# A two-block transformer on one core: paired small experts in the mixture, an early bias table, and the value product of the key memory turned round

## The chip, the cores and the metric

One core of one Trainium2 chip runs the whole program. The metric is the device time of one execution in microseconds (us). Three executions were timed, and one was profiled. TensorE does the matrix products (PE in the profile, PEld its weight loads), VectorE (DVE) and ScalarE (ACT) the elementwise work, GpSimd (POOL) small things and gathers, SyncE (SP) starts most transfers.

## What is computed

512 tokens of width 1024 go through two blocks. Block 1: modulation and norm, input products, retention and differential attention, output product, then a mixture of 32 experts (width 512), of which each token goes to two, weighted by its gates:

```python
for expert e, its tokens x:
    y = (silu(x @ w_gate[e]) * (x @ w_up[e])) @ w_down[e]
    out[token] += gate * y
```

Block 2: norm, a windowed attention with 8 heads, to whose scores a table of biases by relative position is added, a pooling branch, an output product, and last a key memory of 16384 entries with vectors u and v:

```python
a = gelu(h @ u.T) * weight      # weight is 0 but for the chosen entries
out = x + a @ v
```

## The kernel before, in words

Data is fp32. An operand of a large product is cut in two parts, `hi` (rounded to the type fp32r of TensorE) and `lo` (the rest), and three products are summed: hi·hi, hi·lo and lo·hi. A weight comes in chunks of 128x1024 (512 KB) through one ordered list (`add`, from L612). The class `Stream` (`pump`, L338) starts each chunk's load on SP's queue as soon as one of the raw buffers is free (L352), and a given number of chunks ahead of use ACT copies the `hi` part (L363) and DVE subtracts the `lo` part (L365). Each of these engines works through its instructions in order, so an engine that waits for a chunk holds everything behind it. The eight PSUM banks go through `B.get` and `B.put`. Work beside the large products is written as generators (`side`): each `tick` inside a product lets up to two of them go one step.

The helpers are `mm` and `mmx` (products, L522 and L526), `tt` (L529), `stt` (L532), `ts` (L536, L538), `acp` (a copy or function on ACT, L541) and `tr` (a transpose on TensorE, L544). In the profile every use of a helper has its line.

**Block 1's output product** (from L1196) multiplies in chunks (`go(MG, ev_x1, j)`). Beside it run the generators `shift_rows` (pushed at L1230) and `rows_of`, one for each finished tile, which uses ACT and TensorE. Meanwhile `Stream` loads and cuts the first chunks of the experts.

**The mixture** (L1463 to L1690) ranks experts by their number of tokens; rank z is a place. `block_rows(z)` (L119) is a bound on the tokens of a place: 128 for places 0 and 1 and for 29 to 31 (which have two such blocks), between 40 and 128 for the others. `STEPS` (L111) gives the order: by falling rank, with the three large places at steps 6, 13 and 20. A step is `gate_up` (8 chunks), `turn` of the next place (its token rows transposed, split), `down` of the place before (4 chunks), `turn_a`. The token rows are the stationary operand and the weight moves, 512 columns a time: 72 products for each block of rows, however few the rows. `scatter` (L1522) scales the result by the gates (`gtab`) and writes it to memory through POOL.

**The start of block 2** (L1700 to L1785). `band_bias` (L1765) multiplies the bias table by a 0/1 matrix of buckets, and POOL writes the 8x511 result to memory, each row 128 times (L1771, `lb_d`, 2 MB). POOL then reads it back with a pitch that shifts each row by one (L1773, `bmv`), and DVE adds the band mask ten ticks on. `norms` (L1700) needs POOL too, for a power of the norm's statistics (L529 by way of `power`).

**The key memory's product** (L2400 to L2500) goes by 32 groups of 512 entries (`SEQ` is their order), for the first 384 tokens; the other 128 tokens are done by gathers on POOL and sums on DVE (L2291, L2308, L532). For half of the groups `a` is held from an earlier stage, for the other half `u_block` makes it here (24 products of 384 columns for 128 entries, then Gelu on ACT); `weigh` multiplies by the weights and splits. `v_group` (L2437) has the v chunk stationary and the tokens moving: in each half of the width four banks collect 4 blocks of 128 entries, 96 products of 384 columns a group, and DVE adds each of the 8 banks to `X4` (which holds x and becomes the output).

## Time and profile before

| | us |
|---|---|
| median of three timed executions | 2932.4 (2931.6 to 2934.65) |
| the profiled execution, its own time | 2930.98 |
| its span, first to last instruction | 2929.2 |
| PE busy in the span | 2726.5 (93%) |
| DVE busy | 2238.9 (76%) |
| ACT busy | 1262.3 (43%) |
| POOL busy | 757.6 (26%) |

How to read the rows below. A row of the timeline has the start in us, the duration, engine, line and operation, output and inputs, shape and count, and in brackets how long the engine was idle before and what it waited for. A row of the view by line has the busy time, the mean ns of one instruction, and the idle time before them with what ended it. [...] A row of the view of waits has who waited for whom: us in total, times, longest. Pipelined products overlap in their ends, so the time that one adds is read from the distance of two starts.

### The profile page before, as it was taken

The numbers are of one execution on the slowest core, as the hardware profiler recorded it, in microseconds if no ns is written. First come the engines' busy times: TensorE is split into PE (matmuls) and PEld (weight loads), VectorE is DVE, ScalarE is ACT, GpSimd is POOL, SyncE is SP. The second block draws the span as 40 slices with busy tenths as digits, with TensorE's granted clock in tenths as the row PEclk, the third lists the DMA queues.
The fourth block names the chain that finished last, engine by engine and source line by source line (L and its number), as shares of the span: only waits on it lengthen the run. The fifth ranks groups of instructions, "written<-read, shape, count | busy, mean of one in ns | idle before, by whom it ended". The sixth has DMA issues, their size and how long they took to land.

```text
span 2929.2 us, 40594 instructions
## 1 busy us (share of the span) xinstructions
PE 2726.5 (93%) x14351; PEld 2342.7 (80%) x14351; DVE 2238.9 (76%) x4096; ACT 1262.3 (43%) x1859; POOL 757.6 (26%) x669
## 2 busy tenths in 40 slices
PE   6999999988999999985799988999999999999999
PEld 5887888877877665544567888899899999999999
DVE  7554566548898878863558998999688888888887
ACT  3432344345676766751334233444333333333332
POOL 6110021111212111101424555222132332333231
PEclk8999999998999999996899999999999999999999
DMA  6546322347998989975223335888989989999895
GB/s 221 165 124 208 130 73 72 119 140 248 351 323 320 341 305 334 353 247 113 68 69 113 97 118 186 294 293 295 306 296 300 306 287 311 296 297 312 283 304 187
DMA packets 242211, 673.83 MB, mean 230 GB/s; under 512 B 26497, under 2 KB 94513, under 8 KB 238288
## 3 DMA queue, kind: packets, MB, share of 16 engines
q1 hardware_dynamic: 176224, 467.14, 47.3%
q0 software_dynamic: 48256, 156.44, 15.9%
q10 hardware_dynamic: 17520, 47.57, 4.5%
q8 instruction: 115, 1.88, 0.3%
q14 instruction: 96, 0.79, 0.1%
HBM read 625.27 MB, written 62.06 MB: 235 GB/s over the span
## 4 chain that ended last, share of the span: by engine, by line
PE 49%; DVE 29%; DMA 7%; issue 7%; ACT 7%; POOL 1%; ACTq 0%; DVEq 0%; POOLq 0%; SPq 0%
PE bank L522 44%; DVE lo L365 7%; DVE arena L529 6%; DVE arena L532 4%; ACT hi L363 4%; DVE arena L2308 3%; PE bank L526 3%; PE bank L544 2%; DVE arena L538 2%; DVE arena_r L529 2%; ACT arena_r L541 2%; DMA lb_d<-arena 2%; DMA raw<-in_w_in_dram 1%; DMA raw<-in_w_ret_o_dram 1%; ACT arena L541 1%
## 5 line engine op out<-in xcount | busy, mean ns | idle before, releaser
L522 PE MATMUL bank<-arena_r,hi 128*128 128x384 f32 (+1 forms) x5792 | 1618.5, 360 | 42.0 <-DVE arena L529 29.0
L522 PEld LDWEIGHTS bank<-arena_r,hi 128*128 128x128 f32 x5792 | 1066.6, 192 | 123.2 <-issue 39.0
L522 PE MATMUL bank<-arena_r,lo 128*128 128x384 f32 (+1 forms) x2896 | 1032.1, 356 | 22.3 <-POOL lo L365 15.9
L365 DVE TENSOR_TENSOR lo<-raw,hi 128x1024 fp32r<-128x1024 f32 x490 | 602.7, 1242 | 219.9 <-ACT hi L363 215.1
L522 PEld LDWEIGHTS bank<-arena_r,lo 128*128 128x128 f32 x2896 | 554.2, 191 | 65.0 <-POOL lo L365 18.5
L363 ACT ACTIVATE hi<-raw 128x1024 fp32r<-128x1024 f32 x513 | 523.5, 1051 | 176.7 <-DMA raw<-in_v_dram 56.4
L541 ACT ACTIVATE arena<-bank 128x512 f32<-128x512 f32 (+7 forms) x478 | 251.2, 535 | 569.6 <-PE bank L522 437.7
L522 PE MATMUL bank<-hi,arena_r 128*128 128x512 f32 (+10 forms) x1064 | 346.2, 396 | 7.5 <-DVEq L2548 6.2
L541 ACT ACTIVATE arena_r<-arena 128x384 fp32r<-128x384 f32 (+1 forms) x160 | 87.5, 547 | 495.1 <-DVE arena L529 447.9
L529 POOL TENSOR_TENSOR arena<-arena 128x512 f32<-128x512 f32 (+10 forms) x172 | 180.8, 1069 | 380.3 <-ACT arena L541 274.3
L2291 POOL DMA_INDIRECT arena<-in_ur_dram,idx_i x128 | 156.0, 1219 | 401.0 <-DVE arena L2308 393.4
L2291 POOL DMA_INDIRECT arena<-in_vr_dram,idx_i x128 | 157.2, 1228 | 362.6 <-DVE arena L532 337.5
L522 PE MATMUL bank<-arena_r 128*128 128x512 f32 (+12 forms) x956 | 232.9, 398 | 4.4 <-DVE arena_r L538 4.4
L522 PEld LDWEIGHTS bank<-hi,arena_r 128*128 128x128 f32 (+10 forms) x1064 | 161.5, 152 | 89.9 <-issue 7.9
L529 DVE TENSOR_TENSOR arena<-arena,bank 128x384 f32<-128x384 f32 (+6 forms) x314 | 167.9, 570 | 72.3 <-PE bank L522 72.1
L522 PE MATMUL bank<-lo,arena_r 128*128 128x512 f32 (+10 forms) x532 | 209.2, 393 | 1.3 <-DVE lo L365 1.3
L522 PEld LDWEIGHTS bank<-arena_r 128*128 128x128 f32 (+10 forms) x956 | 151.4, 162 | 70.9 <-issue 4.3
L1530 POOL DMA_INDIRECT y_d<-arena,dst_i x34 | 53.0, 1558 | 502.1 <-ACT hi L363 212.4
L529 DVE TENSOR_TENSOR arena_r<-arena,arena_r 128x384 fp32r<-128x384 f32 (+1 forms) x160 | 94.6, 591 | 103.4 <-ACT arena_r L541 103.3
L532 DVE SCALAR_TENSOR_TENSOR arena<-arena 128x1024 f32<-128x1024 f32 (+3 forms) x136 | 165.5, 1217 | 0.2
L2308 DVE SCALAR_TENSOR_TENSOR arena<-arena 128x1024 f32<-128x1024 f32 x128 | 156.0, 1219 | 0.0
L529 DVE TENSOR_TENSOR arena<-arena 128x384 f32<-128x384 f32 (+8 forms) x272 | 125.3, 481 | 23.6 <-DMA arena<-g_d 9.9
(171 smaller groups left out, 2827.1 us busy)
## 6 DMA issues: line engine op xcount, KB each, us to landing
raw<-in_u_dram SPq DMA_DIRECT2D x128, 512.0 KB
raw<-in_v_dram SPq DMA_DIRECT2D x128, 512.0 KB
raw<-in_w_down_dram SPq DMA_DIRECT2D x72, 512.0 KB
raw<-in_w_gate_dram SPq DMA_DIRECT2D x70, 512.0 KB
raw<-in_w_up_dram SPq DMA_DIRECT2D x68, 512.0 KB
arena<-in_w_up_dram SPq DMA_DIRECT2D x60, 512.0 KB
arena<-in_w_gate_dram SPq DMA_DIRECT2D x58, 512.0 KB
raw<-in_w_in_dram SPq DMA_DIRECT2D x57, 512.0 KB
```

Source lines behind the costliest of these rows:

```text
L363: self.nc.scalar.activation(h, r, AF.Copy)
L365: e.tensor_tensor(l, r, h.bitcast(F32), op=OP.subtract)
L522: pe.matmul(ps, l, r, start=start, stop=stop)
L526: pe.matmul(ps, l, r, start=start, stop=stop, skip_group_check=True)
L529: e.tensor_tensor(o, x, y, op=op)
L532: dve.scalar_tensor_tensor(o, x, s, y, op0=op0, op1=op1)
L538: (e or dve).tensor_scalar(o, x, s1, s2, op0=op0, op1=op1)
L541: act.activation(o, x, f, **kw)
L544: pe.transpose(ps, x, kk("ident")[:n, :n])
L1530: i = pool.indirect_dma_start(out=y_d[:], out_offset=IOA(ap=dst_i[:r, z:z + 1], axis=0), in_=y[:r], in_offset=None, bounds_check=2 * S - 1 ...
L2291: pool.indirect_dma_start(out=b, out_offset=None, in_=a[tab], in_offset=IOA(ap=idx_i[:, j:j + 1], axis=0))
L2308: dve.scalar_tensor_tensor(b, b, 1.0, h3, op0=OP.mult, op1=OP.mult, accum_out=s_[:, j:j + 1])
```

## The change

Four things change.

1. The order of the places: after 0 and 1, places of few and of many tokens take turns, `STEPS` is [0, 1, 14, 2, 15, 3, 31, 16, 4, 17, 5, 18, 6, 19, 30, 7, 20, 8, 21, 9, 22, 10, 23, 29, 11, 24, 12, 25, 13, 26, 27, 28]; before it was 0 to 5, 31, 6 to 11, 30, 12 to 17, 29, 18 to 28.
2. The 15 places 14 to 28 get a block of exactly 64 rows, and `hi` and `lo` of the rows stand side by side as 128 columns of the stationary operand. For a piece of a chunk there are two products in place of three. The two halves of the result's 128 rows are added by `fold` (eight small products) behind the gate and up products, and by DVE in `scatter`.
3. The bias table is made in block 1's output product (`bias_rows`, ahead of `shift_rows` among the generators), and the 2 MB write to `lb_d` goes on SP's queue. Block 2 only reads it back, on ACT's queue.
4. In the key memory's product the tokens are stationary and v moves, 512 columns a time: 72 products of 512 columns a group. Six banks hold the output of the 384 tokens through all 32 groups, and two banks are left for `u_block`. x goes into the banks first (`residual_in`, 24 products with the identity, from `x4_d` loaded on ACT's queue). The 8 adds of a group are gone; at the end 6 banks are copied out. Rows of v are laid out in their own order, and the output's layout changes with it.

```diff
 NG = 32
 SEQ = _order()
 RG = 8
...
     if z < NSTAT or z >= NE - NBIG:
         return P
-    return min(P, -(-(2 * S // (z - NSTAT + NBIG + 1)) // RG) * RG)
+    r = min(P, -(-(2 * S // (z - NSTAT + NBIG + 1)) // RG) * RG)
+    return r if r > HB else HB
+
+
...
+    put("fold", (p % HB)[:, None] == np.arange(HB)[None, :])
...
+        def bias_rows():
+
+            lrow, relb = get(), sm(8)
+            nc.sync.dma_start(lrow[:32, :511], a["buckets"])
+            nc.sync.dma_start(relb[:32], a["relb"])
+            for _ in range(4):
+                yield
+            ps = B.get()
+            mm(ps[:8, :511], relb[:32], lrow[:32, :511], True, True)
+            yield
+            acp(lrow[:8, :511], ps[:8, :511])
+            B.put(ps)
+            pool.memset(lrow[:8, 511:512], 0.0)
+            yield
+            nc.sync.dma_start(lb_d[:], lrow[:8, :].unsqueeze(1).to_broadcast([8, P, 512]))
+            lrow.put()
+
         xg = [get(2, True) for _ in range(3)]
...
-        side.push(shift_rows())
+        side.push(bias_rows(), shift_rows())
         ss, lg = B.get(), B.get()
 
...
+        def beside(o, x, n):
+
+            v = o.rearrange("p (q k r) -> p q k r", k=2, r=HB)
+            x = x.rearrange("p (q r) -> p q r", r=HB)
+            acp(v[:, :, 0, :], x)
+            tt(dve, v[:, :, 1, :], x, v[:, :, 0, :].bitcast(F32), OP.subtract)
+
+        def mm_pair(ps, x, wh, wl, first, last):
+
+
+            mmx(ps, x, wh, first, last)
+            mmx(ps[:HB], x[:, :HB], wl, False, last)
+
...
+
+                ps = B.get()
+                for q in range(KT):
+                    tr(ps[:, q * r:(q + 1) * r], x[:r, q * P:(q + 1) * P], r)
+                t = getr(2)
+                beside(t.ap, ps, KT)
+                B.put(ps)
+                xts[z] = t
+                return
...
+        def gate_up_pair(z):
+            x = xts.pop(z)
+            t = []
+            for k in range(2):
+                ps = B.get()
+                for q in range(4):
+                    j, wh, wl = W.get()
+                    for s in range(2):
+                        i = 2 * q + s
+                        c = slice(512 * s, 512 * s + 512)
+                        mm_pair(ps, x[:, i * P:(i + 1) * P], wh[:, c], wl[:, c], i == 0, i == KT - 1)
+                    W.done(j)
+                    tick()
+                y = get()
+                if k:
+                    dve.tensor_copy(y.ap, ps)
+                else:
+                    acp(y.ap, ps)
+                B.put(ps)
+                t.append(y)
+            x.put()
+            act_t[z] = t
+
...
+                    for q in range(4):
+                        o = (4 * k + q) * r
+                        mm(ps[:, o:o + r], y[:, q * P:(q + 1) * P], kk("fold"), True, True)
+                    y.put()
+                y, o = get(), getr()
+                acp(y[:, :256], ps[:, :256], AF.Silu)
+                tt(dve, y[:, :256], y[:, :256], ps[:, 256:], OP.mult)
+                B.put(ps)
+                beside(o.ap, y[:, :256], 4)
+                y.put()
+                aT[z] = o
+                return
             for q in range(4):
                 tr(ps[:, q * r:(q + 1) * r], t[:r, q * P:(q + 1) * P], r)
             t.put()
...
-            ts(y[:r, 512:], o[1][:r], gtab[:r, z:z + 1])
+            if paired(z):
+                for n in range(2):
+                    c = y[:r, 512 * n:512 * n + 512]
+                    acp(c, o[n][HB:], AF.Copy, scale=gtab[HB:, z:z + 1])
+                    stt(c, o[n][:r], gtab[:r, z:z + 1], c, OP.mult, OP.add)
+            else:
+                acp(y[:r, :512], o[0][:r], AF.Copy, scale=gtab[:r, z:z + 1])
+                ts(y[:r, 512:], o[1][:r], gtab[:r, z:z + 1])
...
         bmv = bm.ap.rearrange("p (h c) -> p h c", h=8)
-        onb, relb, lrow, band = get(), get(), get(), get()
-        nc.scalar.dma_start(onb[:32, :511], a["buckets"])
-        nc.scalar.dma_start(relb[:32, :8], a["relb"])
+        band = get()
+        lb = lb_d[:]
+        nc.scalar.dma_start(bmv, bass.AP(tensor=lb.tensor, offset=lb.offset + 127,
+                                         ap=[[511, P], [P * 512, 8], [1, 256]]))
         nc.scalar.dma_start(band[:, :256], a["band"])
         sk = sm(8)
...
-            ps = B.get()
-            mm(ps[:8, :511], relb[:32, :8], onb[:32, :511], True, True)
-            pool.memset(lrow[:8, 511:512], 0.0)
-            acp(lrow[:8, :511], ps[:8, :511])
-            B.put(ps)
-            pool.dma_start(lb_d[:], lrow[:8, :].unsqueeze(1).to_broadcast([8, P, 512]))
-            lb = lb_d[:]
-            pool.dma_start(bmv, bass.AP(tensor=lb.tensor, offset=lb.offset + 127,
-                                        ap=[[511, P], [P * 512, 8], [1, 256]]))
-            yield
             for _ in range(10):
                 yield
             tt(dve, bmv, bmv, band[:, :256].unsqueeze(1).to_broadcast([P, 8, 256]), OP.add)
-            put([onb, relb, lrow, band])
+            band.put()
             ready.append(1)
 
...
+        for n in range(2):
+            nc.scalar.dma_start(xl[n].ap, flat(x4_d[:, 4 * n:4 * n + 4]))
         eslot = get(3, tight=True).ap
...
+
+        acc = [[B.get() for _ in range(2)] for _ in range(ND // P)]
+
+        def residual_in():
+
+            for t, bs in enumerate(acc):
+                for q in range(KT):
+                    x = xl[q // 4][:, q % 4 * ND + t * P:q % 4 * ND + t * P + P]
+                    mmx(bs[q // 4][:, q % 4 * P:q % 4 * P + P], x, kk("ident"), q % 4 == 0, False)
+                tick()
+            put(xl)
+
+        def v_block(x, last):
+
+            c = W.get()
+            for t in range(ND // P):
+                xh, xl_ = (z[:, t * P:(t + 1) * P] for z in x)
+                for n in range(2):
+                    h, l = (z[:, n * 512:n * 512 + 512] for z in c[1:])
+                    ps = acc[t][n]
+                    mmx(ps, xh, h, False, False)
+                    mmx(ps, xl_, h, False, False)
+                    mmx(ps, xh, l, False, last)
+                    if last:
+                        y = get()
+                        if n:
+                            acp(y.ap, ps)
+                        else:
+                            dve.tensor_copy(y.ap, ps)
+                        oc = t * D + n * 512
+                        (nc.sync, nc.scalar)[n].dma_start(out[:, oc:oc + 512], y.ap)
+                    if not (n and t == 1):
+                        if (t, n) != (2, 1):
+                            tick()
+            W.done(c[0])
+            put(x)
 
         load_gate(0)
         load_ge()
...
             if i == 0:
-                for n in range(2):
-                    nc.sync.dma_start(X4[n], flat(x4_d[:, 4 * n:4 * n + 4]))
+                residual_in()
...
-                v_group(w_c, i == NG - 1)
+                for b, x in enumerate(w_c):
+                    v_block(x, i == NG - 1 and b == 3)
```

## Rows read from the trace of the kernel before

**Rows 1.** The page: busy time of the engines, and the chain that ended last.

```profile
PE 2726.5 (93%) x14351; PEld 2342.7 (80%) x14351; DVE 2238.9 (76%) x4096; ACT 1262.3 (43%) x1859; POOL 757.6 (26%) x669
...
PE 49%; DVE 29%; DMA 7%; issue 7%; ACT 7%; POOL 1%; ACTq 0%; DVEq 0%; POOLq 0%; SPq 0%
```

**Rows 2.** [...]

```profile
675.00:1313.00 638.00, 627.72 (x2951) 422.21 (x2950) 532.82 (x567) 447.32 (x554) 107.92 (x101) 0.99 0.88 319
696.00:1236.00 540.00, 540.00 (x2556) 373.71 (x2554) 461.59 (x480) 386.58 (x480) 100.07 (x90) 1.00 0.90 332
...
912.00:948.00 36.00, 36.00 (x176) 28.15 (x175) 24.46 (x28) 19.68 (x26) 10.20 (x4) 1.00 0.75 272
...
1164.00:1200.00 36.00, 36.00 (x171) 18.76 (x170) 32.34 (x35) 26.85 (x34) 4.01 (x6) 1.00 0.98 359
```

**Rows 3.** The timeline of TensorE in two steps of small places.

```profile
1176.93 5.71 PE L522 MATMUL bank<-arena_r 128*48 128x512 f32 x24
...
1182.57 0.69 PE L544 MATMUL bank<-kc,arena 40*128 40x40 f32 x8
...
1200.46 0.69 PE L544 MATMUL bank<-kc,arena 40*128 40x40 f32 x8
```

**Rows 4.** By line and form, DVE in the mixture.

```profile
L365 DVE TENSOR_TENSOR lo<-raw,hi 128x1024 fp32r<-128x1024 f32 x137 | 162.1, 1220 | 27.4 <-ACT hi L363 22.7 <-DVEq L2548 4.0
...
L529 DVE TENSOR_TENSOR arena_r<-bank,arena_r 128x512 fp32r<-128x512 f32 x39 | 25.1, 684 | 4.7 <-ACT arena_r L541 4.7
...
L529 DVE TENSOR_TENSOR arena_r<-bank,arena_r 128x160 fp32r<-128x160 f32 x18 | 5.2, 317 | 0.0
...
L536 DVE TENSOR_SCALAR arena<-bank,arena 40x512 f32<-40x512 f32 x5 | 3.7, 736 | 0.0
...
L529 DVE TENSOR_TENSOR arena_r<-bank,arena_r 128x256 fp32r<-128x256 f32 x6 | 2.3, 416 | 0.1
```

**Rows 5.** The waits, 1335 to 1395 us.

```profile
POOL arena L1773 <- DMA lb_d<-arena: 45.1, 1, 45.1
...
PE bank L522 <- DVE arena L536: 27.0, 1, 27.0
```

**Rows 6.** A window within that wait.

```profile
1366.40:1389.20 22.80, 0.00 (x0) 0.00 (x0) 0.00 (x0) 0.00 (x0) 0.00 (x0) 0.57 0.47 64
```

**Rows 7.** The timeline in block 1's output product: SP's queue, then ACT.

```profile
599.88 7.97 SPq L352 DMA_DIRECT2D raw<-in_w_gate_dram  x4
...
611.49 2.94 ACT L363 ACTIVATE arena_r<-raw 128x1024 fp32r<-128x1024 f32 x3
...
618.65 0.60 ACT L541 ACTIVATE arena<-bank 128x512 f32<-128x512 f32 x1 [3.09 <-PE bank L544]
```

**Rows 8.** A window of the key memory's product, 26 of its 32 groups.

```profile
2164.90:2851.90 687.00, 661.45 (x3744) 657.42 (x3744) 594.93 (x844) 226.29 (x319) 214.69 (x177) 0.99 0.91 300
```

**Rows 9.** The waits of TensorE, 2080 to 2930 us.

```profile
PE bank L522 <- DVE arena L529: 29.0, 13, 3.6
```

**Rows 10.** The timeline of TensorE there: even running, and one wait.

```profile
2400.40 0.33 PE L522 MATMUL bank<-arena_r,lo 128*128 128x384 f32 x1
...
2430.04 0.33 PE L522 MATMUL bank<-arena_r,lo 128*128 128x384 f32 x1
...
2484.57 0.59 PE L522 MATMUL bank<-arena_r,hi 128*128 128x384 f32 x2 [3.23 <-DVE arena L529]
```

**Rows 11.** By line and form, DVE in the same stretch.

```profile
L529 DVE TENSOR_TENSOR arena<-arena,bank 128x384 f32<-128x384 f32 x256 | 129.2, 547 | 7.8 <-PE bank L522 7.8
```

**Rows 12.** By line and form, small fp32 products of TensorE in block 2.

```profile
L522 PE MATMUL bank<-arena_r,arena 128*128 128x128 f32 x768 | 106.1, 281 | 16.2 <-DVE arena L538 15.4 <-ACT arena L541 0.5
```

**Rows 13.** The timeline of ACT there, two Gelu behind a split.

```profile
2443.93 0.53 ACT L541 ACTIVATE arena_r<-arena 128x384 fp32r<-128x384 f32 x1 [7.94 <-DVE arena L529]
...
2445.30 0.47 ACT L541 ACTIVATE arena<-bank 128x384 f32<-128x384 f32 x1
...
2449.69 0.47 ACT L541 ACTIVATE arena<-bank 128x384 f32<-128x384 f32 x1
```

More of the change, by code (lines that the diff above doesn't have):

```diff
@@ L107 @@
 ORDER2 = [4, 5, 0, 1, 2, 3, 9, 8, 7, 6]
-BIG_AT = [6, 13, 20]
-STEPS = list(range(NE - NBIG))
-for _k, _i in enumerate(BIG_AT):
-    STEPS.insert(_i, NE - 1 - _k)
+BIG_AT = [6, 14, 23]
 NG = 32
@@ L116 @@
 RG = 8
+HB = P // 2
 def block_rows(z):
@@ L122, in block_rows, with _steps, paired @@
         return P
-    return min(P, -(-(2 * S // (z - NSTAT + NBIG + 1)) // RG) * RG)
+    r = min(P, -(-(2 * S // (z - NSTAT + NBIG + 1)) // RG) * RG)
+    return r if r > HB else HB
+def _steps():
+    few = [z for z in range(NSTAT, NE - NBIG) if block_rows(z) == HB]
+    many = [z for z in range(NSTAT, NE - NBIG) if block_rows(z) > HB]
+    o, m = list(range(NSTAT)), 0
+    for i, z in enumerate(few):
+        o.append(z)
+        while m < min(len(many), len(many) * (i + 1) // (len(few) - 3)):
+            o.append(many[m])
+            m += 1
+    o.remove(few[-1])
+    o.append(few[-1])
+    for k, i in enumerate(BIG_AT):
+        o.insert(i, NE - 1 - k)
+    return o
+STEPS = _steps()
+PAIR0, PAIR1 = (f(z for z in range(NE) if block_rows(z) == HB) for f in (min, lambda x: max(x) + 1))
+def paired(z):
+    return block_rows(z) == HB
 def _konst():
@@ L651, in build @@
             add(U[4 * SEQ[i + 1]:4 * SEQ[i + 1] + 4])
-        add([flat(a["v"][g, s, m]) for s in range(2) for m in range(2)])
+        add([a["v"][4 * g + b] for b in range(4)])
     W = Stream(nc, chunks, raws, his, los, 0)
@@ L1477, in body @@
         act_t = {}
+        def gate_up_pair(z):
[20 more added lines that the diff above has]
+            act_t[z] = t
         def gate_up(zs):
+            if paired(zs[0]):
+                return gate_up_pair(zs[0])
             xs = [xts.pop(z) for z in zs]
@@ L1513, in turn_a @@
             r = block_rows(z)
+            if paired(z):
+                for k, y in enumerate(t):
+                    for q in range(4):
[10 more added lines that the diff above has]
+                return
             for q in range(4):
@@ L1542, in down @@
                 j, wh, wl = W.get()
-                for (hi, lo), ps in zip(xs, o):
+                for xp, ps in zip(xs, o):
+                    hi, lo = (None, None) if paired(zs[0]) else xp
+                    if paired(zs[0]):
+                        for n in range(2):
+                            c = slice(512 * n, 512 * n + 512)
+                            mm_pair(ps[n], xp[:, i * P:(i + 1) * P], wh[:, c], wl[:, c], i == 0, i == 3)
+                        continue
                     x, y = hi[:, i * r:(i + 1) * r], lo[:, i * r:(i + 1) * r]
@@ L1552, in down @@
             for x, ps, z in zip(xs, o, zs):
-                put(x)
+                if paired(z):
+                    x.put()
+                else:
+                    put(x)
                 if direct and zs == of(STEPS[-1]):
@@ L1565, in add_back @@
             r = block_rows(z)
+            pair = z < NE and paired(z)
+            if pair:
+                r = P
             for n in range(2):
@@ L2408, in body @@
         gslot = [get(6, tight=True).ap for _ in range(2)]
-        X4 = [get(3, tight=True).ap for _ in range(2)]
+        xl = [get(3, tight=True) for _ in range(2)]
+        for n in range(2):
+            nc.scalar.dma_start(xl[n].ap, flat(x4_d[:, 4 * n:4 * n + 4]))
         eslot = get(3, tight=True).ap
@@ L2435, in weigh @@
             return h, l
-        def v_group(ws, last):
-            for s in range(2):
-                bs = [B.get() for _ in range(4)]
-                for m in range(2):
-                    c = W.get()
-                    for d in range(4):
-                        ps = bs[d][:, :ND]
-                        for b in range(2):
-                            o = b * 512 + d * P
-                            h, l = c[1][:, o:o + P], c[2][:, o:o + P]
-                            xh, xl = (x[:, :ND] for x in ws[2 * m + b])
-                            mm(ps, h, xh, m + b == 0, False)
-                            mm(ps, h, xl, False, False)
-                            mm(ps, l, xh, False, m + b == 2)
-                        tick()
-                        if m:
-                            o = X4[s][:, d * ND:(d + 1) * ND]
-                            tt(dve, o, o, ps, OP.add)
-                            B.put(bs[d])
-                            if last:
-                                oc = (4 * s + d) * ND
-                                (nc.sync, nc.scalar)[d % 2].dma_start(out[:, oc:oc + ND], o)
-                    W.done(c[0])
-            for x in ws:
-                put(x)
@@ new lines, in body @@
+        acc = [[B.get() for _ in range(2)] for _ in range(ND // P)]
[10 more added lines that the diff above has]
+                xh, xl_ = (z[:, t * P:(t + 1) * P] for z in x)
+                for n in range(2):
+                    h, l = (z[:, n * 512:n * 512 + 512] for z in c[1:])
[7 more added lines that the diff above has]
+                            acp(y.ap, ps)
+                        else:
+                            dve.tensor_copy(y.ap, ps)
[5 more added lines that the diff above has]
+            W.done(c[0])
+            put(x)
```

12 lines of the change are left out of this document (7 added, 5 removed).

## The prediction

> **What bounds the kernel now.** The page comes first: TensorE is busy for 93% of the span and takes 49% of the chain that ended last, DVE 29% [rows 1]. So I read TensorE's gaps, and where it has none, whose work stands close behind it.
>
> In the mixture TensorE never pauses for 540 us [rows 2], yet DVE is not far off: in two steps of small places it is busy 32.34 of 36 us, and the DMA engines 0.98 of the time, while in a step of a large place (912 to 948) both drop, to 24.46 us and 0.75 [rows 2]. So three resources stand nearly level, and the large places are where the other two idle.
>
> At the start of block 2 TensorE stands still for 27.0 us behind a DVE operation; the same view shows the cause one row up, POOL waiting 45.1 us for its write of the bias table before it can do the norm's power [rows 5]. In the middle of it no engine does anything, half of the DMA engines' time is used, and the granted clock is 0.57, next to the lower of its two levels [rows 6].
>
> In the key memory's product TensorE is busy 661.45 of 687 us [rows 8], but a little of that is slow running: the even pitch is 0.1733 us a product (171 products from 2400.40 to 2430.04 [rows 10]), and 3744 products at that pitch are 649 us. So 38 us in 26 groups are lost, and 47 in 32. The waits for DVE's adds to free a bank make 29.0 us in 13 waits [rows 9]; the rest is lower clock after them and single gaps.
>
> **The sum** is made against the profiled execution's own 2931.0 us, 1.4 below the median of the three.
>
> **Paired places.** 24 products take 5.64 us (1176.93 to 1182.57 [rows 3]), 0.235 each. 15 places lose 24 of their 72: 15 x 24 x 0.235 = 85 us. Eight folds by place stand against four transposes; eight small ones take 0.69 us [rows 3], so about 0.5 us a place, 8 in all. TensorE's work falls from 628 to some 550 us. What is late next: a step lasts 17.89 us (1182.57 to 1200.46), and DVE's part of it is 32.34 x 17.89 / 36 = 16.1 us [rows 2, 3], twelve splits of 1.22 at the core of it [rows 4]. The change takes from DVE in a paired step two subtractions of 128x160 (0.32 each), a multiplication over 512 columns (0.68 by the nearest row), a third subtraction (0.32) and a scaling (0.74), 2.4 us; it adds a subtraction and a copy of 128x512 (0.68 each), two operations of 128x256 (0.42 each) and two scalings of 64x512 (0.74 each), 3.7 us [rows 4]. So 17.4 us: a paired step is bounded by DVE, and gains 0.5 us on the 17.89, 15 x 0.5 = 8. The rest of the gain has to come from the three large steps, where DVE idles 11.5 of 36 us and the DMA engines 9 [rows 2]: now that small places take turns with them and with middling ones, whose 17.9 us of products leave DVE 1.8, the buffers drained before can be refilled there. I take 8 us for each, a little under the nearer of the two limits: 24. Together **-32**. Bounds: 10, where only the paired steps gain; 44, from 0.90 of 540 us of DMA time done at the 0.98 seen [rows 2].
>
> The gathers and scatters of 64 rows in place of 40 lie on POOL, of which 108 of 638 us are used [rows 2]: nothing. The new order as such moves the same work.
>
> **Bias table, block 2.** Without its write, POOL does the power at once and TensorE's 27.0 us go; what is late next is the norm's own chain, which was on time for everything but POOL. With some 2 us of running at the lower clock behind the pause: **-29** (bounds 24 and 31). The read back goes to ACT's queue at the block's start, far ahead of the add; ACT only issues it.
>
> **Bias table, block 1.** The write needs 46 us wherever it is put, as long as half of the engines carry it [rows 5, 6]. Now it is issued from SP, in the generator's seventh step, that is by four ticks to a chunk in the second chunk of the output product, near 593 us (an estimate), ahead of the four expert loads of 599.88 on the same queue [rows 7]. If these stand behind it, they land at about 640, and ACT, which split them at 611.49 [rows 7], waits for 28 us. Behind ACT's splits stand the copies of finished tiles, and TensorE's next transposes need them; ACT waits 3.09 us for TensorE after them, so the slack is small [rows 7]: I take 2 to 3 us off and add 2 for the clock, **+28**. Bounds: 0, if the loads pass, and 30. I take the upper end because the nearest row shows the write slow whatever the other queues do, while a quick pass would need the free half of the engines to carry whole chunks.
>
> The other instructions of that step move with it, from one stretch with TensorE full to another: the table's small product, its copy on ACT, a memset on POOL. They cost there what they save later. Its two small loads go on SP ahead of the write, under a tenth of a megabyte, where four chunks of 512 KB take 7.97 us to issue [rows 7]: under 1 us. The generator holds one of the two places for side work while it lasts, so the first `rows_of` starts later; the drain at the end of the product covers it, or costs at most a tile's worth, which I count at nothing.
>
> [...]
>
> **Key memory.** The turned product itself is worth nothing to TensorE: 96 x 0.1733 = 16.64 us a group before [rows 10], 72 x 0.231 = 16.64 after (0.231 is 0.1733 x 512 / 384). What goes is 256 adds of DVE, 0.505 us each in pitch (129.2 us [rows 11]), and with them the wait for a bank. Of the 47 us lost I take 35: with none lost the DMA engines would have to go from 0.91 to 0.91 x 687 / 649 = 0.96, close to the highest share seen, and some gaps must stay. `residual_in` puts 24 fp32 products on TensorE, 0.138 (106.1 / 768) to 0.281 us each [rows 12]: 3.3 to 6.7 us; they follow one another as in that row's own runs, so 3. Its input, 1.5 MB, leaves SP's queue for ACT's and comes earlier; SP's v chunks gain what ACT's queue pays, nothing net. **-32** net; bounds 12 and 43. At the end six banks are copied out beside each other where two adds were: within 1 us.
>
> Sum: 2931.0 - 32 - 29 + 28 - 32 = **2866 us**.
>
> **The rivals.**
> *The write holds nothing up.* If the transfer is faster from SP, or the loads pass it, the 28 us stay away: 2866 - 28 = 2838. For it: half of the engines' time is free. Against: the write alone took 46 us with nothing beside it on that queue. Chance 0.22.
>
> *DVE and the transfers are already the bound.* The mixture then gives its 10 and the key memory 12: 2931 - 10 - 29 + 28 - 12 = 2908. For it: DMA shares of 0.98 and 0.91 [rows 2, 8]. Against: both stages have stretches in which DVE and DMA idle. Chance 0.15.
>
> *Slower: two banks in place of many.* In `u_block` the products of one 128 entries may start only when the Gelu of the second before has left its bank. Here ACT's queue is the place: Gelu stands behind a split that waited 7.94 us for DVE [rows 13]. Two Gelu lie 4.39 us apart, a block's products take 24 x 0.1733 = 4.16, so there is no spare. At w us of wait for each of the 64 blocks the price is 64 x w on top of 2866, and the change is slower from w = 65 / 64, about 1 us; at 2 us it is 2994. Against: the late DVE work was the adds of banks, which go, and DVE's load in the 687 us falls from 595 to 595 - 208 x 0.505 = 490. Chance 0.05.
>
> **How the numbers follow.** The forecast has 0.50, the three rivals 0.42, and 0.08 stays for mixtures between, mostly in sum still faster. The likeliest case spans about 2850 to 2885 by its own bounds; the range takes in the first rival and the second, 2832 to 2908, and leaves out the two-bank case and the far ends. A measurement of this kernel can tell some 0.2%, 6 us. Only the two-bank case, or several dear terms together, reaches no change: faster 0.92, same 0.03, slower 0.05.
>
> **What would show each step.** In the mixture's windows, TensorE no longer full, DVE at 95% or more, the stretch near 606 us instead of 638; if DVE is below 90% there, the term is wrong. No idle window of 20 us at the start of block 2. In block 1's output product, ACT waiting some 25 us for a load of `w_gate`: its absence makes the second term of the bias wrong. In the key memory, no wait of TensorE for a DVE add, and 64 Gelu as the new place to look at; a wait of TensorE there of 1 us a block would make the whole forecast wrong.

## The result, and the profile after

The changed kernel takes 2850.1 us (median of four runs, 2847.0 to 2852.2) against 2933.5 us for the one before (four runs, 2931.6 to 2936.5). The ratio is 0.9714, 95% interval 0.9697 to 0.9731: 83 us faster. The forecast was 2866, 65 us faster, with a range of 2832 to 2908 that holds the result. The profiled execution of the changed kernel took 2852.2 us, span 2850.4; it was the slowest of its four, so between the two profiled executions the difference is 78.8 us of span, and the table below explains those.

To see where it went, the span is cut at three events that both kernels have: the first small product of the gates' table (early in the mixture), the last scatter of the mixture, the first u product behind the last gate matrix of the key memory, and then the last product of all. The timeline of the kernel before, TensorE and POOL:

```profile
681.43 0.49 PE L522 MATMUL bank<-arena_r,arena 128*128 128x128 f32 x2
...
1308.42 1.32 POOL L1530 DMA_INDIRECT y_d<-arena,dst_i  x1 [21.62 <-DMA raw<-in_w_down_dram]
...
2063.12 0.99 PE L522 MATMUL bank<-arena_r,hi 128*128 128x384 f32 x2
...
2924.57 0.34 PE L522 MATMUL bank<-arena_r,lo 128*128 128x384 f32 x1
```

And of the changed kernel (its helpers have moved by some lines: `mm` is L549, `mmx` L553, `tt` L556, `stt` L559, `ts` L563 and L565, `acp` L568, the splits L390 and L392):

```profile
706.01 0.49 PE L549 MATMUL bank<-arena_r,arena 128*128 128x128 f32 x2
...
1301.81 0.91 POOL L1643 DMA_INDIRECT y_d<-arena,dst_i  x1 [23.11 <-DVE arena L559]
...
2026.73 0.99 PE L549 MATMUL bank<-arena_r,hi 128*128 128x384 f32 x2
...
2845.74 0.39 PE L553 MATMUL bank<-lo,arena_r 128*128 128x512 f32 x1
```

| stretch | before, us | after, us | difference | forecast |
|---|---|---|---|---|
| start to the gates' table (block 1's output product) | 681.4 | 706.0 | +24.6 | +28 |
| to the last scatter (mixture) | 627.0 | 595.8 | -31.2 | -32 |
| to the first u product (block 2, bias) | 754.7 | 724.9 | -29.8 | -29 |
| to the last product (key memory) | 861.5 | 819.0 | -42.4 | -32 |

The page of the changed kernel, where [rows 1] had its first line:

```profile
PE 2657.1 (93%) x13453; PEld 2246.4 (79%) x13453; DVE 2136.1 (75%) x3858; ACT 1287.4 (45%) x1876; POOL 876.4 (31%) x667
```

TensorE has 69 us less to do and DVE 103. The chain that ended last breaks off on its way back in this profile, so it isn't set against [rows 1].

In block 1's output product ACT now waits for a load of `w_gate`, and TensorE for ACT. The timeline of ACT, then the waits of 580 to 700 us:

```profile
635.28 1.06 ACT L390 ACTIVATE arena_r<-raw 128x1024 fp32r<-128x1024 f32 x1 [23.07 <-DMA raw<-in_w_gate_dram]
```

```profile
PE bank L553 <- ACT arena L568: 23.0, 2, 21.5
...
```

At the start of block 2 the pause is gone: TensorE's longest wait between 1303 and 1395 us is 3.1 us, where [rows 5] had 27.0 in one. The first two rows of the view:

```profile
PE bank L571 <- POOL arena L556: 4.0, 2, 2.6
PE bank L549 <- ACT arena_r L568: 3.1, 1, 3.1
...
```

The mixture and the key memory, by windows. A row has the stretch and its length in us, the busy time of PE, PEld, DVE, ACT and POOL with the number of instructions in brackets, the granted TensorE clock as a share of full speed, the busy share of the 16 DMA engines, and GB/s; the rows of [rows 2], [rows 6] and [rows 8] are built the same way.

```profile
700.00:1308.00 608.00, 580.25 (x2768) 431.92 (x2768) 543.65 (x582) 463.15 (x568) 197.19 (x104) 0.98 0.90 335
...
1060.00:1230.00 170.00, 165.96 (x814) 118.13 (x813) 156.53 (x167) 134.24 (x167) 65.52 (x31) 1.00 0.93 351
```

```profile
2100.00:2800.00 700.00, 700.00 (x3411) 620.28 (x3410) 549.22 (x689) 253.57 (x347) 260.12 (x194) 1.00 0.93 320
```

In the middle of the mixture (1060 to 1230 us) TensorE has small gaps now, with DVE at 0.92 and the DMA engines at 0.93, where [rows 2] had no gap in 540 us; in the key memory it has none in 700 us, at a granted clock of 1.00, where [rows 8] had 661 of 687. The waits of TensorE there, 2020 to 2851 us, against 29.0 us in 13 waits in [rows 9]:

```profile
PE bank L549 <- ACT arena L568: 8.2, 1, 8.2
PE bank L549 <- DVE arena L565: 2.4, 1, 2.4
```

### The profile page after: what moved, and what is told of

It is laid out like the page before. It is cut to its first block, busy times and chain, and to the rows that moved or that the text cites. A ratio compares the mean times of both kernels' runs of the same rounds, so it can differ in the third digit from the quotient of the medians.

```text
span 2850.4 us, 38447 instructions
## 1 busy us (share of the span) xinstructions
PE 2657.1 (93%) x13453; PEld 2246.4 (79%) x13453; DVE 2136.1 (75%) x3858; ACT 1287.4 (45%) x1876; POOL 876.4 (31%) x667
## 4 chain that ended last, share of the span: by engine, by line
PE 36%; DVE 13%; issue 2%; DMA 2%; POOL 1%; ACT 1%; ACTq 0%; another core or an unknown queue 0%; POOLq 0%; DVEq 0%
PE bank L553 19%; PE bank L549 17%; DVE arena L565 2%; DVE arena L556 2%; DVE lo L392 2%; DVE arena L559 1%; DVE arena_r L556 1%; DVE arena L2252 1%; DVE arena L2259 1%; DVE arena L2254 1%; DVE arena L2318 1%; DMA arena<-g_d 1%; POOL arena L556 1%; ACT arena L568 1%; DMA arena<-y_d 1%
## 5 line engine op out<-in xcount | busy, mean ns | idle before, releaser
L549 PE MATMUL bank<-arena_r,hi 128*128 128x384 f32 (+1 forms) x3744 | 1087.1, 371 | 18.3 <-ACT arena L568 8.2
L392 DVE TENSOR_TENSOR lo<-raw,hi 128x1024 fp32r<-128x1024 f32 x490 | 601.3, 1241 | 227.0 <-ACT hi L390 219.2
L549 PEld LDWEIGHTS bank<-arena_r,hi 128*128 128x128 f32 x3744 | 690.3, 192 | 94.5 <-ACT arena L568 8.6
L549 PE MATMUL bank<-arena_r,lo 128*128 128x384 f32 (+1 forms) x1872 | 685.7, 366 | 21.4 <-POOL lo L392 16.6
L553 PE MATMUL bank<-hi,arena_r 128*128 128x512 f32 (+1 forms) x2216 | 663.7, 375 | 23.9 <-ACT arena_r L568 12.9
L390 ACT ACTIVATE hi<-raw 128x1024 fp32r<-128x1024 f32 x513 | 526.1, 1052 | 239.4 <-DMA raw<-in_v_dram 78.4
L568 ACT ACTIVATE arena<-bank 128x512 f32<-128x512 f32 (+6 forms) x496 | 259.8, 533 | 650.4 <-PE bank L549 500.2
L553 PEld LDWEIGHTS bank<-hi,arena_r 128*128 128x128 f32 x2216 | 410.8, 193 | 110.2 <-ACT arena_r L568 14.9
L553 PE MATMUL bank<-lo,arena_r 128*128 128x512 f32 (+2 forms) x1224 | 462.7, 378 | 11.8 <-DVE lo L392 11.6
L549 PEld LDWEIGHTS bank<-arena_r,lo 128*128 128x128 f32 x1872 | 357.6, 191 | 64.5 <-POOL lo L392 19.2
L556 POOL TENSOR_TENSOR arena<-arena 128x512 f32<-128x512 f32 (+10 forms) x172 | 180.8, 1069 | 382.6 <-ACT arena L568 273.9
L553 PEld LDWEIGHTS bank<-lo,arena_r 128*128 128x128 f32 (+1 forms) x1224 | 223.4, 183 | 61.5 <-DVE lo L392 21.9
L568 ACT ACTIVATE arena_r<-arena 128x384 fp32r<-128x384 f32 (+2 forms) x175 | 93.7, 535 | 333.1 <-DVE arena L556 323.9
L549 PE MATMUL bank<-hi,arena_r 128*128 128x512 f32 (+6 forms) x608 | 198.0, 396 | 0.0
L556 DVE TENSOR_TENSOR arena_r<-arena,arena_r 128x384 fp32r<-128x384 f32 (+2 forms) x175 | 101.1, 578 | 109.9 <-ACT arena_r L568 109.7
L559 DVE SCALAR_TENSOR_TENSOR arena<-arena 128x1024 f32<-128x1024 f32 (+3 forms) x136 | 166.6, 1225 | 14.0 <-DMA arena<-in_vr_dram,idx_i 13.6
L556 DVE TENSOR_TENSOR arena<-arena 128x384 f32<-128x384 f32 (+8 forms) x272 | 127.2, 489 | 42.3 <-ACT arena L568 24.8
L549 PE MATMUL bank<-arena_r 128*128 128x512 f32 (+8 forms) x560 | 137.4, 399 | 3.2 <-DVE arena_r L565 3.2
```

The costliest lines, as they stand in the source:

```text
L390: self.nc.scalar.activation(h, r, AF.Copy)
L392: e.tensor_tensor(l, r, h.bitcast(F32), op=OP.subtract)
L549: pe.matmul(ps, l, r, start=start, stop=stop)
L553: pe.matmul(ps, l, r, start=start, stop=stop, skip_group_check=True)
L556: e.tensor_tensor(o, x, y, op=op)
L559: dve.scalar_tensor_tensor(o, x, s, y, op0=op0, op1=op1)
```

## Experiments: the write of the bias table

Each kernel below is an edit of the changed kernel. The kernel before ran beside them (medians 2929.4 to 2931.1 us), so ratios to it are compared: the changed kernel's is 0.9714, and a difference in us between two kernels is the difference of their ratios times 2930.

**The write from 128 partitions.**

```diff
+            dve.tensor_copy(wide8[:32, :P].rearrange("p (h k) -> p h k", k=16),
+                            relb[:32].unsqueeze(2).to_broadcast([32, 8, 16]))
-            mm(ps[:8, :511], relb[:32], lrow[:32, :511], True, True)
+            mm(ps[:, :511], wide8[:32, :P], lrow[:32, :511], True, True)
...
-            nc.sync.dma_start(lb_d[:], lrow[:8, :].unsqueeze(1).to_broadcast([8, P, 512]))
+            nc.sync.dma_start(lb_d[:].rearrange("h (k c) x -> (h k) c x", k=16),
+                              lrow.ap.unsqueeze(1).to_broadcast([P, 8, 512]))
```

> The bias table is made for 128 rows (16 copies of each head), so that the write to memory starts from 128 partitions, 8 copies each, and is cut among all 16 DMA engines; same bytes, same queue, same place. Theory (the write holds the loads behind it because half of the engines carry it for 44 us): the write takes 6 to 15 us, ACT no longer waits 23.07 us for the load of w_gate, and the time falls by 20 to 26 us from 2850, to some 2826. Rival (any write of 2 MB ahead of the loads delays them; the span of the pause is memory's own): a wait of over 15 us stays and the time is within 8 us of 2850.

2825.5 us (2818.4 to 2828.2), ratio 0.9641 [0.9625, 0.9657]: 21 us less than the change by the ratios. Its profile, the part on transfers from 584 to 650 us (last column: median us from issue to landing), and the splits of `w_gate` on ACT, which no longer wait:

```profile
raw<-in_w_gate_dram SPq DMA_DIRECT2D x8, 512.0 KB, 4.1
lb_d<-arena SPq DMA_DIRECT2D x1, 2048.0 KB, 8.9
```

```profile
608.90 2.94 ACT L390 ACTIVATE arena_r<-raw 128x1024 fp32r<-128x1024 f32 x3
```

In the changed kernel the loads of `w_gate` in the same stretch took 29.3 us in the median, and while the write of 8 partitions ran by itself the DMA engines were 0.44 busy (7.0 of 16 engines' time); during this one they are 0.93 busy. The changed kernel's rows first, then this kernel's window:

```profile
raw<-in_w_gate_dram SPq DMA_DIRECT2D x4, 512.0 KB, 29.3
...
592.00:598.00 6.00, 6.00 (x36) 5.23 (x35) 1.78 (x3) 5.22 (x8) 0.00 (x0) 1.00 0.44 51
```

```profile
590.00:600.00 10.00, 10.00 (x68) 9.00 (x68) 4.35 (x5) 5.04 (x7) 0.00 (x0) 1.00 0.93 333
```

The same 2 MB land after 8.9 us, and ACT's wait of 23.07 us is gone. The theory holds: the shape of the transfer made it slow. The share of 0.44, and of 0.47 in [rows 6], can be read as half of the engines carrying the write, though no view shows which engines carry a transfer. But the share only doubles, while the write takes 8.9 us where the one of 8 partitions took 45.1 in [rows 5]: the number of busy engines alone does not account for that.

**The same write on POOL's queue.**

```diff
-            nc.sync.dma_start(lb_d[:], lrow[:8, :].unsqueeze(1).to_broadcast([8, P, 512]))
+            pool.dma_start(lb_d[:], lrow[:8, :].unsqueeze(1).to_broadcast([8, P, 512]))
```

> The write of 8 partitions goes on POOL's queue in place of SP's, at the same step of block 1. [...] Rival (the eight engines are simply full for 44 us, the queue is indifferent): the wait stays above 20 us and the time at 2850 within 5.

2840.0 us, ratio 0.9691 [0.9675, 0.9708]: 7 us less than the change. If a queue of their own let the loads pass beside the write, I expected 10 to 18 us less and 5 to 10 us of wait on ACT in place of 23. The two intervals overlap a little, but the profile has the gain where it belongs: the gates' table starts at 699.15 us, 6.9 before that of the change. The transfers of its profile, 584 to 650 us, and ACT's splits:

```profile
raw<-in_w_gate_dram SPq DMA_DIRECT2D x5, 512.0 KB, 26.1
lb_d<-arena POOLq DMA_DIRECT2D x1, 2048.0 KB, 44.5
...
arena<-in_xT_dram POOLq DMA_DIRECT2D x2, 256.0 KB, 45.1
```

```profile
618.31 1.06 ACT L390 ACTIVATE arena_r<-raw 128x1024 fp32r<-128x1024 f32 x1 [7.33 <-DMA raw<-in_w_gate_dram]
624.37 1.06 ACT L390 ACTIVATE arena_r<-raw 128x1024 fp32r<-128x1024 f32 x1 [5.00 <-DMA raw<-in_w_gate_dram]
630.40 1.06 ACT L390 ACTIVATE arena_r<-raw 128x1024 fp32r<-128x1024 f32 x1 [4.97 <-DMA raw<-in_w_gate_dram]
```

From another queue the first load gets through earlier, and one wait of 23.07 us becomes three of 17.3 us in sum. So the queue matters, but is worth only 7 us: beside the write the loads still take 26.1 us, against 29.3 behind it. Two small loads of 256 KB that POOL issued right after the write took 45.1 us.

**The table back in block 2.** The code of before for this part alone.

```diff
-        side.push(bias_rows(), shift_rows())
+        side.push(shift_rows())
...
+            pool.dma_start(lb_d[:], lrow[:8, :].unsqueeze(1).to_broadcast([8, P, 512]))
```

> The bias table is made and written in block 2 again, as before; the three other parts stay. Theory: the pause of 27 us at the start of block 2 comes back, the one of 21.5 us in block 1 goes; the time is 2850 plus 3 to 9. Rival (the early table was the gain of the change at the block boundary): plus 25 to 30.

2851.9 us, ratio 0.9730 [0.9714, 0.9746]: 5 us more than the change by the ratios, whose intervals overlap. The profile shows why: the gates' table starts 24 us earlier than in the change, and at the start of block 2 the pause is back:

```profile
PE bank L549 <- DVE arena L563: 23.7, 1, 23.7
```

So the early table as such was worth some 5 us: it moved a pause. Early and wide it is worth 26 us against this kernel. No run has the wide write in block 2's old place, so how much of the 26 needs the early place is not shown.

## Experiments: the mixture

**Pairs in the old order.**

```diff
+STEPS = list(range(NE - NBIG))
+for _k, _i in enumerate([6, 13, 20]):
+    STEPS.insert(_i, NE - 1 - _k)
```

> Paired places stay, the order of the places is the one before (large places at steps 6, 13, 20, then small ones in a row). Theory (small paired steps in a row are bound by DVE's 17.4 us each, and TensorE's saving can be used only where long steps stand between): 15 to 28 us slower than 2850, DVE over 0.95 busy in the run of small places at the end. Rival (pairs alone give the gain, the order is indifferent): within 6 us of 2850.

2863.6 us, ratio 0.9789 [0.9763, 0.9815], 22 us more than the change. The last scatter and the windows of the run of small places at the end:

```profile
1318.76 0.90 POOL L1627 DMA_INDIRECT y_d<-arena,dst_i  x1 [24.37 <-DMA raw<-in_w_down_dram]
```

```profile
1060.00:1230.00 170.00, 158.33 (x760) 114.30 (x758) 156.75 (x169) 133.57 (x168) 28.86 (x30) 0.96 0.92 341
```

TensorE falls to 158 of 170 us there, with DVE at 0.92, not the 0.95 expected. With the gates' table at 702.7 us, the mixture takes 616 us: pairs alone give 11 of the 31 us. TensorE's waits in it sum to 35.5 us, against 24.7 in the changed kernel and 10.2 in the kernel before.

**The new order without pairs.** `paired` is false everywhere and `block_rows` as before.

```diff
 def paired(z):
-    return block_rows(z) == HB
+    return False
```

> The new order stays, all places are computed as before (three products, their own number of rows). Theory (the order moves the same work and TensorE is full): 28 to 34 us slower than 2850, TensorE without a pause in the mixture. Rival (the order alone evens out DVE and transfers): 10 us slower or less.

2882.7 us, ratio 0.9841 [0.9823, 0.9858], 37 us more, a little over the theory's 34. Its last scatter and the same window:

```profile
1331.39 0.91 POOL L1623 DMA_INDIRECT y_d<-arena,dst_i  x1 [22.36 <-DMA raw<-in_w_down_dram]
```

```profile
1060.00:1230.00 170.00, 170.00 (x811) 110.96 (x809) 143.74 (x153) 119.02 (x151) 26.65 (x27) 1.00 0.89 330
```

TensorE is full again and the mixture, from 703.1 us on, takes 628: the order alone gives nothing. The two together give 31, so 20 of them come from the order letting pairs be used. As I read it, the saving of TensorE pays only where DVE and the transfers can catch up; the waits of 35.5 and 24.7 us fit that.

**The copies of the up product on ACT.**

```diff
-                if k:
-                    dve.tensor_copy(y.ap, ps)
-                else:
-                    acp(y.ap, ps)
+                acp(y.ap, ps)
```

> In the paired places the copy of the up product's bank goes from DVE to ACT: 15 x 0.7 us less on DVE, as much more on ACT, which was 0.78 busy. Theory (DVE is the bound of the mixture after the change): 5 to 10 us faster than 2850. Rival (the transfers at 0.93 of their engines are the bound, or the small waits at the steps' ends are): within 4 us.

2843.3 us, ratio 0.9711 [0.9695, 0.9727]: by the ratio the same as the change. In the profile the mixture is 590.6 us long (705.80 to 1296.36), 5 less. Some of that seems real, since the other kernels here with the same pairs and order have 593 to 596, and the last one below, with the copies on ACT too, 589.1; but it is less than the times can tell. TensorE itself is busy for 569 of the 596 us in the changed kernel; what holds up the rest, DVE or the transfers, stays open.

## Experiments: the key memory

**The product as before.** `v_group`, the order of v and the output of before.

```diff
-                for b, x in enumerate(w_c):
-                    v_block(x, i == NG - 1 and b == 3)
+                v_group(w_c, i == NG - 1)
```

> The key memory's product as before (v stationary, banks freed by DVE adds); the three other parts stay. Theory: the waits for DVE adds and the slow stretches after them come back, 2850 plus 38 to 44. Rival (the stage was bound by its transfers, and gained from the later start): plus 15 or less.

2888.2 us, ratio 0.9855 [0.9838, 0.9871], 41 us more; the waits, 2045 to 2885 us, are those of [rows 9] again:

```profile
PE bank L549 <- DVE arena L556: 29.5, 14, 3.6
PE bank L549 <- ACT arena_r L568: 2.3, 2, 1.6
```

**Eight adds without banks.** DVE gets as much to do as before, on a spare tile; no bank waits for it.

```diff
+                    for _ in range(2):
+                        tt(dve, spare[:, :ND], spare[:, :ND], spare[:, :ND], OP.add)
                     v_block(x, i == NG - 1 and b == 3)
```

> In the key memory's product eight adds of 128x384 on a spare tile are put back on DVE in each group, so DVE's load is again that of before, but no bank waits for them. Theory (the gain of 41 us came from the waits for banks that DVE freed late): within 6 us of 2850. Rival (DVE's load itself was the bound, through late weighing and splits): 15 to 40 us slower.

2892.5 us, ratio 0.9872 [0.9855, 0.9888], 46 us more: my theory fell, and the loss is even above the rival's 40. The waits (2090 to 2890 us), the window, and ACT around one of the waits:

```profile
PE bank L549 <- ACT arena L568: 30.9, 13, 6.1
```

```profile
2100.00:2800.00 700.00, 673.29 (x3199) 592.68 (x3198) 614.72 (x862) 230.52 (x323) 215.83 (x181) 0.98 0.88 299
```

```profile
2404.77 0.52 ACT L568 ACTIVATE arena_r<-arena 128x384 fp32r<-128x384 f32 x1 [8.12 <-DVE arena L556]
2405.20 1.04 ACT L390 ACTIVATE hi<-raw 128x1024 fp32r<-128x1024 f32 x1
2406.15 0.47 ACT L568 ACTIVATE arena<-bank 128x384 f32<-128x384 f32 x1
```

Thirteen waits of 30.9 us take the place of the 13 waits of 29.0 in [rows 9], for another reason: the Gelu at 2406.15 stands behind a split that waited 8.12 us for DVE, and its bank is one of the two that `u_block` has. That is the two-bank rival of the prediction, seen with its price. So in the turned form, with DVE as busy as before, the gain is gone.

**Four adds.** As above with one add in place of two per block of 128 entries.

> As with the eight spare adds a group in the key memory's product, but four. Theory (the stage slows once DVE runs late, by a slack): less than a third of the 45 us that eight cost, 5 to 15 us over 2850. Rival (each us of DVE's work costs its share): 20 to 25 us over 2850.

2846.5 us, ratio 0.9720 [0.9699, 0.9742]: no cost that the ratio can tell, where even the theory expected 5 to 15. The window:

```profile
2100.00:2800.00 700.00, 700.00 (x3402) 619.25 (x3401) 597.11 (x802) 254.01 (x347) 224.26 (x194) 1.00 0.92 319
```

DVE at 597 of 700 us leaves TensorE full; the stage, from the first u product to the last product, takes 818 us as with none (819), and 864 with eight. So the price is not one per us; it looks like a threshold between four and eight adds. My reading, which no run tests by itself, is that DVE has to be back from its burst of splits and weighing before a bank is wanted.

**The product as before, splits on POOL.** To the kernel with `v_group` one line is added, by which every third `lo` split of the stage goes to POOL.

```diff
         W.ahead = AH_V
+        W.turns = 3
```

> The key memory's product as before, adds and bank waits kept, but every third split of a weight chunk goes from DVE to POOL: some 85 x 1.22 us less on DVE, as many x 2.5 us more on POOL. Theory (the stage was held up by DVE running late, whichever wait showed it): the stage falls from 861 us to 820 to 840, TensorE's waits for DVE's adds below 10 us in sum. Rival (the adds' place in DVE's order, behind the weighing, makes the wait, however much DVE has to do): within 8 us of the kernel with the product as before, 2888.

2951.9 us, ratio 1.0073 [1.0056, 1.0090], 64 us over the kernel with the product as before; the stage takes 921 us (2026.81 to 2948.18). It doesn't decide between the theories, since DVE was not relieved: it is busy for 607.0 of the 700 us from 2150 to 2850, as in the kernel with the product as before (607.8 from 2120 to 2820), while TensorE gets through fewer products. The waits of TensorE, 2000 to 2955 us, then the view by line and form, 2150 to 2850 us, and a meeting of DVE and POOL in the timeline:

```profile
PE bank L549 <- DVE arena L556: 67.4, 30, 5.2
```

```profile
L392 DVE TENSOR_TENSOR lo<-raw,hi 128x1024 fp32r<-128x1024 f32 x99 | 145.0, 1464 | 19.5 <-ACT hi L390 19.5
L559 DVE SCALAR_TENSOR_TENSOR arena<-arena 128x1024 f32<-128x1024 f32 x85 | 132.6, 1560 | 6.0 <-DMA arena<-in_vr_dram,idx_i 6.0
```

```profile
2414.95 2.46 POOL L392 TENSOR_TENSOR lo<-raw,hi 128x1024 fp32r<-128x1024 f32 x1 [10.35 <-ACT hi L390]
2415.10 3.39 DVE L2428 SCALAR_TENSOR_TENSOR arena<-arena 128x1024 f32<-128x1024 f32 x1
```

A split on DVE takes 1464 ns here on the mean, 1220 in [rows 4], and a scaled sum with two inputs 1560, 1279 in the kernel before. The last two rows have both engines at once: the other kind of scaled sum, 1218 ns each in the kernel before, takes 3.39 us where it starts 0.15 us after a split on POOL. So a split that is moved saves DVE 1.2 us and can cost it 2.2.

**x loaded late.** The 1.5 MB of x are issued after the first group and put into the banks just before the first v product.

```diff
-        for n in range(2):
-            nc.scalar.dma_start(xl[n].ap, flat(x4_d[:, 4 * n:4 * n + 4]))
...
+            if i == -1:
+                for n in range(2):
+                    nc.scalar.dma_start(xl[n].ap, flat(x4_d[:, 4 * n:4 * n + 4]))
```

> The 1.5 MB of x for the key memory's banks are loaded after the first group has been made, and put into the banks just before the first v product; before that, two loads of 768 KB ran beside the first gate and held-table loads, which landed after 18.3 and 19.9 us. Theory (that one wait of TensorE, 8.24 us for a Gelu behind a split that waited for the gate load, is due to the x loads): it falls to 0 to 3 us, the time by 5 to 9 us (1.6 us were waited before the change). Rival (the gate load is late by itself): the wait stays, within 3 us.

2858.1 us (2848.7 to 2866.2), ratio 0.9757 [0.9728, 0.9786]: not better. The waits, 2000 to 2955 us:

```profile
PE bank L553 <- DMA arena<-x_d: 10.4, 1, 10.4
...
PE bank L549 <- ACT arena L568: 3.3, 1, 3.3
```

The wait of 8.2 us falls to 3.3, just above the 0 to 3 of the theory. That x's loads made it is not shown even so: with the table back in block 2, where x is loaded as in the change, the same wait is 4.0 us. And TensorE now waits 10.4 us for x itself. The timeline of ACT and TensorE there:

```profile
2058.84 1.02 ACTq L2628 DMA_DIRECT2D arena<-x_d  x2
...
2067.17 7.72 PE L553 MATMUL bank<-kc,arena 128*128 128x128 f32 x48 [10.37 <-DMA arena<-x_d]
```

ACT issues the loads only at 2058.84, when TensorE has already stood for 2 us, and they take another 8 us: put off this far in ACT's order, they could not be in time. In the profile the stage takes 825.6 us, 6.6 more than in the change, which the new wait explains; the ratio's 13 us are more, and the rest stays open.

**Three edits together**: the wide write, x late, copies on ACT.

> Three edits together: the write of the table from 128 partitions, x loaded late, the paired copies on ACT. If they add: 21 + 7 + 3 us below the changed kernel, 2815 to 2822, ratio 0.962 or less. Rival (they share a slack, above all the late copies with the earlier start): 2825 to 2830.

2826.2 us, ratio 0.9638 [0.9621, 0.9654]. They don't add: this is the wide write's 0.9641 again. The wide write alone, 21 us faster than the change by the ratios and 105 faster than the kernel before, is as good and the simplest: the best version found.

## Why the prediction was right, and where it was off

Against the profiled execution (2852.2 us) the forecast of 2866 was 14 us too slow: 10 in the key memory, 3 in block 1 and 1 in block 2, with 1 the other way in the mixture.

**Bias table.** Right in both halves: the pause at the start of block 2 went (-29.8, forecast -29), and its cause came along to block 1 (+24.6, forecast +28). There ACT waited 23.07 us. Of the 5 us that miss to the forecast wait of 28, 3 are the estimate of the place in time (the write was issued at 590.05 us, not 593); the rest can't be read apart, since this trace has no landing of the write. The rival "the write holds nothing up" is refuted by that wait, and the wide write shows what the forecast had not looked for: that the 46 us were a matter of shape, not of bytes (8.9 us for the same 2 MB). That loads on the write's queue would come after it was my estimate, which no row of the kernel before shows; here the first of them landed 45 us after the write's issue. The "lower clock behind the pause" was 0.50 in the kernel before from 1389 to 1395 us; what it cost can't be read apart from the 29.8.

**Mixture.** Right in size (-31.2, forecast -32), but partly by luck. The windows of this stretch, before and after:

```profile
681.43:1308.42 626.99, 616.71 (x2908) 415.13 (x2908) 525.41 (x553) 439.49 (x545) 105.27 (x98) 0.99 0.88 321
```

```profile
706.01:1301.81 595.80, 569.18 (x2732) 424.01 (x2732) 534.06 (x565) 453.92 (x557) 193.43 (x98) 0.99 0.91 338
```

The forecast took 78 us of work off TensorE and gave 46 of them back to the bound by DVE. In fact TensorE's busy time fell by 47.5 us only, and its idle time rose by 16.3. Two errors cancelled. One can be named: the eight folds of a place were put at 0.5 us net, but an fp32 product shows as two instructions, and the 16 of a place take 1.89 us:

```profile
1119.10 1.89 PE L549 MATMUL bank<-kc,arena 128*128 128x64 f32 x16
```

That is 28 us in 15 places, some 23 when the transposes that they replace are taken off, where the sum has 8; the rest of the missing work can't be read apart. The other error is that DVE holds TensorE up less than forecast. What I named as its sign was not met: DVE is at 0.92 in the window of 1060 to 1230 us, not 0.95, and over the whole stretch at 0.896, just below the 0.90 at which I wanted to call the term wrong; and relieving DVE brought nothing that the times can tell. TensorE is busy for 0.955 of the stretch, so it is still near its own bound.

The experiments bear out how the gain is put together: 8 us expected from pairs alone, 11 measured; nothing from the order; 24 expected from the two together, 20 measured. That these 20 come in the large steps, as the forecast had it, was not read apart.

**Key memory.** Here the sum was mis-sized by 10 us: "Of the 47 us lost I take 35". 42.4 came net of x's products, which took 5.3 us where the sum has 3: the 24 products are 48 instructions, and the forecast had taken each of the 768 instructions of [rows 12] for a product, and then a value below its own 3.3 to 6.7. So some 48 came back, all that was lost. The reason that I gave for stopping at 35, DMA engines at 0.96, was wrong: TensorE ran without a gap at a share of 0.93. That the turned product itself is worth nothing to TensorE can't be read apart, but the 64 blocks of u fitted between it with one wait in all. The timeline of the changed kernel has x's products, 2067.73 to 2073.00 us, and ahead of them that one wait, a Gelu late behind the gate's load:

```profile
2061.11 1.01 PE L549 MATMUL bank<-arena_r,hi 128*128 128x384 f32 x2 [8.24 <-ACT arena L568]
...
2067.73 5.52 PE L553 MATMUL bank<-kc,arena 128*128 128x128 f32 x48
2073.00 0.70 PE L553 MATMUL bank<-hi,arena_r 128*128 128x512 f32 x2
```

And the mechanism was half right. "What goes is 256 adds of DVE" and "with them the wait for a bank": the runs with spare adds show that in the turned form the adds count as DVE's load, not at four a group but at eight, and that another wait then takes the place of the one for the adds. Whether in the kernel before the load alone would have sufficed, with other banks, is not shown, since the experiment meant for it slowed DVE.

**The slower side.** The two-bank rival was real but switched off by the very adds that went: at four adds a group its price is nothing, at eight 45 us in the stage, some 0.7 us for each of the 64 blocks, under the 1 us at which the forecast saw the whole gain gone.

## What to carry to other kernels

A wait moved to another stage is only moved (here -29.8 us at the start of block 2, +24.6 in block 1): look at why the transfer is long before looking for a place to hide it, and at what stands behind it on its queue and in the engines that it uses. A saving on a full engine pays where the engines behind it have slack, so order the work such that heavy and light steps take turns (here the pairs gave 11 us in the old order and 31 in the new). And load on an engine that is not the bottleneck may cost nothing up to a point, and beyond it a stage's whole gain: here four adds a group cost nothing and eight 45 us.

## What the hardware showed that was not expected

The write of 2 MB from 8 partitions took 44.5 us on POOL's queue, the same bytes from 128 partitions on SP's 8.9 us: five times faster, with the DMA engines' busy share going from 0.44 to 0.93. The queue doesn't explain it: behind the write of 8 partitions on SP's queue the first load landed 45 us after the write's issue (590.05 to 635.28 us). Why each byte takes longer from 8 partitions is not shown.

Splits moved to POOL slowed DVE's own splits by a fifth on the mean (1464 ns against 1220), and single instructions from 1.2 to 3.4 us. The add that reads a bank was not slowed (542 ns, 547 in the kernel before). Of the two other operations of that shape, `arena<-arena` took 840 ns in place of 552 and `arena_r<-arena,arena_r` 559 in place of 560; what decides which is slowed is not shown.

An fp32 product shows as two instructions in the trace: 48 for the 24 products of x, 0.22 us for each product of 128 columns.
